# Transposing x raw at the start and loading the output projection's residual from DRAM

## The chip, the core and the metric

One core of a Trainium2 chip runs the kernel. The metric is the device time of one execution in microseconds (us), as the median of several. TensorE (PE in the profile, PEld for its weight loads) multiplies, VectorE (DVE) and ScalarE (ACT) work on tiles and take products out of PSUM, GpSimd (POOL) works on tiles in SBUF, SyncE (SP) issues most of the DMAs. Each engine runs its own list of instructions in order and waits on semaphores.

## The reference

One decoder layer for a prompt of 512 tokens and 64 sample tokens (8 x 8), 1024 channels wide. The mixer's three branches (gated linear attention, pooling, dilated attention) are merged into one product with w_out, and x itself is added to it:

```python
xn = rmsnorm(x, norm1_g)
(q_g, k_g, v_g, r_g, a_lr, u_pool, q_a, k_a, v_a, g_a, g_b, g_c) = split(xn @ w_in)
...
merged = sigmoid(g_a) * y_a + sigmoid(g_b) * y_b + sigmoid(g_c) * y_c
h = x + merged @ w_out
f, c_new = conv_ffn(rmsnorm(h, norm2_g), conv_prev, ffn_w_up, ffn_conv_w, ffn_conv_b, ffn_w_down)
y = rmsnorm(h + f, final_norm_g)
```

All is float32. The outputs are y, the new states and the new key and value caches.

## The kernel before

**Layout.** Activations lie with channels on partitions: a tile [128, 576] holds 128 channels of all 576 tokens (NT; NP = 512 of them are the prompt's). The inputs x lie with tokens on rows, so x is transposed on TensorE. A float32 product is made of three products of float32r parts: weights' high part (wh) by activations' high (xh), wh by low (xl), low (wl) by xh (`products`, line 199; its matmuls are line 207).

**Weights** come in chunks of up to 512 KB, in order of use. `load` (line 145) issues a chunk's DMA on SP into one of three raw slots (wr), `split` (line 154) casts the high part on ACT (line 161) and subtracts the low part on DVE (line 164), for the first two chunks on POOL. `fetch` (line 193) splits chunks i and i + 1 and loads the two after.

**PSUM.** `big` (line 115) gives one of three banks (tag g) for products, `small` (line 123) one of five for the rest (tags s and h).

**Norm 1** (lines 300 to 363). Five tiles xts[t] of 128 tokens (the last of 64) come in by DMA. For each, ACT squares and sums (line 347), POOL makes the reciprocal root (lines 230 and 231), DVE scales the tile in place in two halves of 512 channels (line 351), TensorE transposes each half in four pieces into one PSUM bank (line 354, against the identity, which is the first piece of the constants ca), ACT casts it to xh (line 357) and DVE subtracts to xl (line 358).

**The gate chain** (lines 446 to 475). The low-rank gate's factors (lines 450 and 453) and the first products of k and q are made for tokens 0 to 255 and then for 256 to 575. Logits follow (line 440); the factors reach them over DVE and ACT (lines 455 to 460). ACT takes exponents and logarithms (lines 470 and 472), DVE running sums (line 475). v's products (line 395) are taken out on DVE (line 400, vs), which stands behind the first two of these sums.

**Output projection** (lines 1098 to 1124). x is loaded a second time (lines 1103 and 1104, xt2). For each of eight tiles m of 128 channels five transposes (lines 1110 and 1111) bring x into PSUM, ACT copies it into x1 (lines 1112 and 1113), 48 products follow, and DVE adds half of each product bank to x1 (line 1115). ACT and DVE then make xh2 and xl2, ACT squares (lines 1117 to 1120), POOL sums.

**What sets the order.** The program is written in one sequence; a scheduler places each engine's instructions at build time, by its own estimates, and sets the waits. DMAs on a hardware queue take eight semaphores in turn, so a DMA also waits until the one eight before it has landed. Tiles with `bufs=n` rotate through n slots; a new tenant waits for the last reader of the old.

Of the kernel before, what the change touches and what calls it, by code (L numbers as in the profile page):

```python
# [18 lines left out]
D = 1024  # L19
# [83 lines left out]
def hybrid_step(ctx: ExitStack, tc: tile.TileContext, I, O, at_a, at_b):  # L103
# [3 lines left out]
    # ---------------------------------------------------------------- pools  # L107
# [7 lines left out]
    def big():  # L115
        return psg.tile([128, 512], F32, tag="g", name="g")
# [19 lines left out]
    # ------------------------------------------------------- weight stream  # L136
# [41 lines left out]
    def side_copy(after):  # L178
        """one of the copies within DRAM, issued behind an instruction of the Pool engine"""
        if copies:  # L180
            dst, src = copies.pop(0)
            with tc.issue_after(after.ins):
                nc.gpsimd.dma_start(dst, src)
# [15 lines left out]
    def products(ps, ids, xh, xl, t0, t1, c=0):  # L199
        """weights' hi and lo against the activations' hi and lo, into ps [128, t1 - t0]"""  # L200
# [9 lines left out]
    def gemm(ids, xh, xl, evac, halves=EVEN, c=0, bank=big):  # L210
        """128 columns of x @ w for all tokens, half of them at a time; evac(psum, t0, t1) takes each half away"""
        for t0, t1 in halves:
            ps = bank()
            products(ps, ids, xh, xl, t0, t1, c)
            evac(ps[:, :t1 - t0], t0, t1)

    def tanh_half(t):
        """sigmoid(x) = (1 + tanh(x / 2)) / 2: the tanh"""
        return lambda ps, t0, t1: S.activation(t[:, t0:t1], ps, AF.Tanh, scale=0.5)

    def gate(t):
        """(1 + tanh) x: twice the gated value"""
# [5 lines left out]
    def power(r, ms, e):  # L228
        """r = (ms + e) ** -0.5, two small tiles of one shape"""
# [3 lines left out]
    # ------------------------------------------------------------ constants  # L233
# [14 lines left out]
    # ------------------------------------------------------------ the plan of weight chunks, in order of use  # L248
# [51 lines left out]
    # --------------------------------------------------------------- norm 1  # L300
# [42 lines left out]
    rs = st.tile([128, 5], F32, name="rs")  # L343
    for t in range(5):
        n = 128 if t < 4 else 64
        junk = st.tile([128, D], F32, tag="junk", name="junk", bufs=1)
# [18 lines left out]
    def packed_sample(pool):  # L365
        """[hi | lo] of the samples' activations, one stationary operand"""
# [5 lines left out]
    def token_major(ids, order, out_p, out_s, tmp, xsp):  # L372
        """x @ w for 256 columns with tokens on partitions; out_p [128, 4, 256], out_s [64, 256]."""
# [32 lines left out]
    # ------------------------------------------------------------------ GLA  # L406
# [11 lines left out]
    # the gate's low-rank factors: [hi | hi | lo] against the activations, then [hi; lo; hi] against [hi; hi; lo]  # L418
# [49 lines left out]
    # log gates (times 16) and their running sums within the chunks  # L468
# [10 lines left out]
    def chunked(t, off_p, off_s):  # L479
        """per-chunk element (64 wide chunks, then the samples' 8 wide) broadcast over its chunk"""  # L480
# [13 lines left out]
    for h in range(4):  # L494
# [42 lines left out]
        # the state runs over pairs of chunks: k to the end of the pair, q from its start  # L537
# [11 lines left out]
        # token-major k for the state updates  # L549
# [6 lines left out]
        # the samples', half of them at a time: [hi; hi; lo] of k against [hi; lo; hi] of v  # L556
# [15 lines left out]
        # within the chunks  # L572
# [8 lines left out]
        # between the chunks of a pair  # L581
# [5 lines left out]
        # states after each pair  # L587
# [12 lines left out]
        # the samples' queries against their states  # L600
# [28 lines left out]
        for d in range(2):  # L629
            def silu(ps, t0, t1):  # L630
                """twice the SiLU"""
# [9 lines left out]
        # norm over the head's 256 values, gate  # L641
# [24 lines left out]
    # ------------------------- GLA's gate and projection, and the pooling branch between them  # L666
# [75 lines left out]
    # ------------------------------------------------- the pooling branch's gate and projection  # L742
# [5 lines left out]
    # the FFN's convolution weights and states, channels on partitions  # L748
# [20 lines left out]
    # ---------------------------------------------------------- attention  # L769
# [19 lines left out]
    def minus_max(out, scores, bias, least):  # L789
        """out = -(scores + bias), and its least"""  # L790
        V.tensor_tensor_reduce(out=out, in0=scores, in1=bias, scale=-1.0, scalar=3e38, op0=OP.add, op1=OP.min, accum_out=least)

    def part_scores(g, heads, t, qT, kT):
        """exp(scores - max) of one block of queries; heads as pairs (p, [hh, hh])"""
# [54 lines left out]
    def scores_by_key(g, bq, sp, qb):  # L849
        """every query of a residue against its keys, features on partitions"""  # L850
# [22 lines left out]
    def scores_by_query(sT, bq):  # L873
        """one query to a residue: its row on all partitions, products and sums along the keys' rows"""
# [18 lines left out]
    def sample_units(g, bq):  # L893
        """the samples' attention of one group and half of the batch, in steps"""
# [68 lines left out]
    for g in GROUPS:  # L963
# [38 lines left out]
        # new rows of the caches  # L1002
# [27 lines left out]
    # weights of the groups: softmax over their log-denominators  # L1030
    def group_weights(mxs, dens, shape, pool, tag):
        """mxs (minus m), dens: [128, X, 3, Y] -> weights over sum p v, e^(m - M) / sum den e^(m - M)"""
# [42 lines left out]
    # ------------------------------------------------------------ merge  # L1075
# [22 lines left out]
    # ----------------------------------------------- output projection, norm 2  # L1098
    x1_cm, x1p = open_pool("x1", "right")
    x1 = x1p.tile([128, 8, NT], F32, name="x1")  # L1100
    xr_cm, xrp = open_pool("xr", "right")
    xt = xrp.tile([128, 5, D], F32, name="xt2")
    nc.sync.dma_start(xt[:, :4, :], xin)
    nc.sync.dma_start(xt[:64, 4, :], I["x_sample"].rearrange("b i d -> (b i) d"))
    xh2 = xpool.tile([128, 8, NT], F32R, tag="xh", name="xh2")
    xl2 = xpool.tile([128, 8, NT], F32R, tag="xl", name="xl2")
    for m in range(8):
        px, px2 = small(), small()
        for t in range(4):
            T.transpose(px[:, 128 * t:128 * t + 128], xt[:, t, 128 * m:128 * m + 128], ident)  # L1110
# [187 lines left out]
```

## Time and profile before

| | |
|---|---|
| timed runs, us | 1327.8, 1327.64, 1325.46 |
| median, us | 1327.64 |
| profiled execution, span from first to last instruction, us | 1324.9 |
| TensorE busy, us | 1305.0 |
| DVE, ACT, POOL busy, us | 601.6, 464.3, 242.4 |
| DMA, mean GB/s | 141 |

The page gives no other time for the profiled execution than its span, which lies 2.7 us under the median of the timed runs. Matmuls are pipelined and their busy time runs from the issue to a modelled end, so two that follow each other overlap in the rows; the distance of their starts is what one costs.

### The profile page before, as it was taken

How to read it: one execution, taken by the hardware profiler on the slowest of the kernel's cores; microseconds unless marked ns; L12 is line 12 of the kernel's file. 1: busy time of each engine (PE TensorE's matmuls, PEld its weight loads, DVE VectorE, ACT ScalarE, POOL GpSimd, SP SyncE). 2: the span in 40 equal slices, each digit the busy share in tenths (PEclk: the TensorE clock that was granted, in tenths of full speed). 3: DMA queues.
4: the chain of work that ended last, by engine and by line, in shares of the span. 5: the costliest groups of instructions: out<-in, count | busy, mean ns of one | idle time of the engine just before them, and what ended most of it. 6: DMA issues, size and time to landing. Idle time of an engine off the chain costs nothing.

```text
span 1324.9 us, 23686 instructions
## 1 busy us (share of the span) xinstructions
PE 1305.0 (99%) x9903; PEld 1257.5 (95%) x9903; DVE 601.6 (45%) x1004; ACT 464.3 (35%) x899; POOL 242.4 (18%) x398
## 2 busy tenths in 40 slices
PE   8899999999999999999999999999999999999997
PEld 6899999999999999998988889999999999999997
DVE  5754564433453333162633366435555555532223
ACT  6554553534321222242433343433222222222223
POOL 4320211022410112041311110122121212200000
PEclk9999999999999999999999999999999999999999
DMA  7232432355443557266676415363455555444333
GB/s 218 65 116 68 144 115 69 96 178 158 131 141 95 163 159 220 73 184 190 182 217 204 154 31 167 100 225 118 145 164 162 162 167 157 148 129 149 91 88 116
DMA packets 220582, 187.44 MB, mean 141 GB/s; under 512 B 7900, under 2 KB 216393, under 8 KB 219700
## 3 DMA queue, kind: packets, MB, share of 16 engines
q1 hardware_dynamic: 218682, 142.28, 36.8%
q0 software_dynamic: 1792, 43.65, 9.6%
q8 instruction: 78, 1.28, 0.4%
q14 instruction: 28, 0.23, 0.1%
q10 hardware_dynamic: 2, 0.00, 0.0%
HBM read 175.52 MB, written 54.27 MB: 173 GB/s over the span
## 4 chain that ended last, share of the span: by engine, by line
PE 94%; DVE 2%; ACT 2%; issue 1%; DMA 1%; POOL 0%; SPq 0%; POOLq 0%; DVEq 0%; ACTq 0%
PE g L207 63%; PE g L1249 8%; PE g L395 8%; PE h L1249 2%; PE h L936 1%; PE s L805 1%; PE s L207 1%; PE s L864 1%; PE s L828 1%; PE s L820 1%; PE s L881 1%; PE h L869 1%; PE s L611 0%; DVE bb L475 0%; PE s L591 0%
## 5 line engine op out<-in xcount | busy, mean ns | idle before, releaser
L207 PE MATMUL g<-xl,wh 128*128 128x288 f32 (+2 forms) x1664 | 494.1, 297 | 0.0
L207 PE MATMUL g<-xh,wh 128*128 128x288 f32 (+2 forms) x1664 | 494.1, 297 | 0.0
L207 PE MATMUL g<-xh,wl 128*128 128x288 f32 (+2 forms) x1664 | 492.8, 297 | 1.1 <-DVE wl L164 1.1
L161 ACT CAST wh<-wr 128x1024 fp32r<-128x1024 f32 (+3 forms) x181 | 184.4, 1019 | 485.8 <-PE g L207 287.8
L164 DVE TENSOR_TENSOR wl<-wr,wh 128x1024 fp32r<-128x1024 f32 (+3 forms) x179 | 227.1, 1268 | 252.9 <-ACT wh L161 252.2
L207 PEld LDWEIGHTS g<-xh,wl 128*128 128x128 f32 x1664 | 313.7, 189 | 3.3 <-issue 1.4
L207 PEld LDWEIGHTS g<-xl,wh 128*128 128x128 f32 x1664 | 314.1, 189 | 2.3 <-issue 2.0
L207 PEld LDWEIGHTS g<-xh,wh 128*128 128x128 f32 x1664 | 314.2, 189 | 1.1 <-issue 0.7
L395 PE MATMUL g<-wh,xh 128*128 128x256 f32 x224 | 72.1, 323 | 2.5 <-DVE vs L400 2.5
L1249 PE MATMUL g<-hh,wl 128*128 128x288 f32 (+2 forms) x286 | 72.2, 297 | 0.0
L1249 PE MATMUL g<-hh,wh 128*128 128x288 f32 (+2 forms) x286 | 72.0, 297 | 0.0
L395 PE MATMUL g<-wl,xh 128*128 128x256 f32 x224 | 71.5, 319 | 0.0
L1249 PE MATMUL g<-hl,wh 128*128 128x288 f32 (+2 forms) x286 | 71.5, 295 | 0.0
L395 PE MATMUL g<-wh,xl 128*128 128x256 f32 x224 | 71.4, 320 | 0.0
L395 PEld LDWEIGHTS g<-wh,xh 128*128 128x128 f32 x224 | 52.3, 233 | 5.7 <-DVE vs L400 2.7
L395 PEld LDWEIGHTS g<-wl,xh 128*128 128x128 f32 x224 | 52.3, 234 | 0.7 <-issue 0.7
L395 PEld LDWEIGHTS g<-wh,xl 128*128 128x128 f32 x224 | 52.4, 234 | 0.0
L1249 PEld LDWEIGHTS g<-hh,wl 128*128 128x128 f32 x286 | 49.8, 189 | 0.0
L1249 PEld LDWEIGHTS g<-hh,wh 128*128 128x128 f32 x286 | 49.6, 189 | 0.0
L1249 PEld LDWEIGHTS g<-hl,wh 128*128 128x128 f32 x286 | 49.6, 189 | 0.0
L1159 DVE TENSOR_TENSOR ae<-g,rst 128x256 f32<-128x256 f32 x44 | 18.6, 425 | 64.0 <-PE g L207 64.0
L226 DVE TENSOR_TENSOR yr<-yr,g 128x288 f32<-128x288 f32 x44 | 18.1, 451 | 49.8 <-POOL yr L1189 49.8
(453 smaller groups left out, 2179.9 us busy)
## 6 DMA issues: line engine op xcount, KB each, us to landing
wr<-in_w_in_dram SPq DMA_DIRECT2D x74, 512.0 KB
wr<-in_ffn_w_up_dram SPq DMA_DIRECT2D x44, 512.0 KB
out_dram<-in_cache_k_w_dram POOLq DMA_DIRECT2D x8, 2040.0 KB, 8.4
out_dram<-in_cache_v_w_dram POOLq DMA_DIRECT2D x8, 2040.0 KB, 8.3
kv<-in_cache_k_w_dram SPq DMA_DIRECT2D x26, 512.0 KB
kv<-in_cache_v_w_dram SPq DMA_DIRECT2D x26, 512.0 KB
wr<-in_ffn_w_down_dram SPq DMA_DIRECT2D x18, 448.0 KB
wr<-in_ffn_w_down_dram SPq DMA_DIRECT2D x9, 512.0 KB
```

Of the source, the lines that this page charges most:

```text
L161: S.copy(hi[:, :n], self.raw[:, :n])
L164: self.cut_at = E.tensor_tensor(lo[:, :n], self.raw[:, :n], hi[:, :n].bitcast(F32), op=OP.subtract)
L207: T.matmul(ps[:, :t1 - t0], a[:, k, c:c + 128], b(n)[:, t0:t1], start=(n == 0 and j == 0), stop=(n == len(ks) - 1 and j == 2))
L226: return lambda ps, t0, t1: V.tensor_tensor(t[:, t0:t1], t[:, t0:t1], ps, op=OP.mult)
L395: mm = T.matmul(dst, a, b[:, n % 4, :], start=(n == 0 and j == 0), stop=(n == 7 and j == len(seq) - 1))
L805: T.matmul(sp[:, nk * n:nk * n + nk], qT[r, p, 128 * t:128 * t + 128], kT[r, p, k0:k0 + nk], start=True, stop=True)
L820: T.transpose(pt[:, 128 * n:128 * n + 128], s4[:, h, 128 * kb:128 * kb + 128], ident)
L828: T.matmul(po[64 * hh:64 * hh + 64, 128 * x:128 * x + 128], vt[:, blocks[kb], 64 * (2 * p + hh):64 * (2 * p + hh) + 64], pts[:, (2 * x + h ...
L864: T.transpose(pk[:, 128 * n:128 * n + 128], kt[:, 2 * half + n // 2, 128 * (n % 2):128 * (n % 2) + 128], ident)
L869: T.matmul(sp[32 * b:32 * b + 32, 0:128], qz[:, p, 32 * b:32 * b + 32], kT[:, n, p, :], start=(r == 0 and p == 0), stop=(r == NR[g] - 1 an ...
L1159: V.tensor_tensor(ae[:, 2 + t0:258 + t0], ps[:, :256], rst[:, t0:t0 + 256], op=OP.mult)
L1249: T.matmul(q[:, :t1 - t0], a[:, k, :], b[n][:, t0:t1], start=(n == 0 and j == 0), stop=(n == NF - 1 and j == 2))
```

## The change

At the start each tile xts[t] is also transposed raw, ahead of its scaling: eight more transposes a tile (line 352 of the new kernel) into two of the three product banks, ACT copies the first half and DVE the second (line 353) into a tile xtr with two slots, and SP writes it to a DRAM scratch xturn of [1024, 576] (line 354). Since the scaling works in place, it waits for the raw transposes of its half. At the output projection the second load of x, its 40 transposes and the 16 copies are gone; x1 is now eight tiles, each loaded from xturn (line 1111 of the new kernel). The arithmetic is the same. The other lines of the diff are removed comments, and x1[:, m, ...] written as x1[m][:, ...].

```diff
@@ norm 1, lines 342 to 348 @@
     ss = st.tile([128, 5], F32, name="ss")
     rs = st.tile([128, 5], F32, name="rs")
+
+    xturn = dpool.tile([D, NT], F32, name="xturn")
     for t in range(5):
         n = 128 if t < 4 else 64
+        xtr = st.tile([128, 8, 128], F32, tag="xtr", name="xtr", bufs=2)
+        for kk in range(2):
+            ps = big()
+            for k in range(4):
+                T.transpose(ps[:, n * k:n * k + n], xts[t][:n, 512 * kk + 128 * k:512 * kk + 128 * k + 128], ident[:n, :n])
+            (V.tensor_copy if kk else S.copy)(xtr[:, 4 * kk:4 * kk + 4, :n], ps[:, :4 * n].rearrange("p (k n) -> p k n", k=4))
+        nc.sync.dma_start(xturn.rearrange("(k p) t -> p k t", p=128)[:, :, 128 * t:128 * t + n], xtr[:, :, :n])
         junk = st.tile([128, D], F32, tag="junk", name="junk", bufs=1)
...
@@ output projection, lines 1098 to 1120 @@
     x1_cm, x1p = open_pool("x1", "right")
-    x1 = x1p.tile([128, 8, NT], F32, name="x1")
+    x1 = [x1p.tile([128, NT], F32, name=f"x1_{m}") for m in range(8)]
+    for m in range(8):
+        nc.sync.dma_start(x1[m], xturn[128 * m:128 * m + 128, :])
     xr_cm, xrp = open_pool("xr", "right")
-    xt = xrp.tile([128, 5, D], F32, name="xt2")
-    nc.sync.dma_start(xt[:, :4, :], xin)
-    nc.sync.dma_start(xt[:64, 4, :], I["x_sample"].rearrange("b i d -> (b i) d"))
     xh2 = xpool.tile([128, 8, NT], F32R, tag="xh", name="xh2")
     xl2 = xpool.tile([128, 8, NT], F32R, tag="xl", name="xl2")
     for m in range(8):
-        px, px2 = small(), small()
-        for t in range(4):
-            T.transpose(px[:, 128 * t:128 * t + 128], xt[:, t, 128 * m:128 * m + 128], ident)
-        T.transpose(px2[:, :64], xt[:64, 4, 128 * m:128 * m + 128], ident[:64, :64])
-        S.copy(x1[:, m, :NP], px)
-        S.copy(x1[:, m, NP:], px2[:, :64])
         gemm(P["out", m], lambda k: ga_h[:, k, :], lambda k: ga_l[:, k, :],
-             lambda ps, t0, t1: V.scalar_tensor_tensor(x1[:, m, t0:t1], ps, 0.5, x1[:, m, t0:t1], op0=OP.mult, op1=OP.add))
+             lambda ps, t0, t1: V.scalar_tensor_tensor(x1[m][:, t0:t1], ps, 0.5, x1[m][:, t0:t1], op0=OP.mult, op1=OP.add))
...
```

The scheduler places the rest. Rows of an engine's list name line, operation, output and inputs, and the shape. On TensorE at the very start, before (xt_93 to xt_97 are the tiles of tokens, s and h banks of `small`, g of `big`, ca the identity):

```order
L340 MATMUL s<-grow,ones 128x512 x2
L354 MATMUL s<-ca,xt_93 128x128 x4
L354 MATMUL h<-ca,xt_94 128x128 x4
L354 MATMUL s<-ca,xt_93 128x128 x4
L354 MATMUL s<-ca,xt_94 128x128 x4
L207 MATMUL g<-xh,wh 128x256
L207 MATMUL g<-xl,wh 128x256
```

And now, from the third tile's scaled transposes on (line 352 is raw, line 363 scaled; ahead of these rows stand line 340 and the earlier transposes):

```order
L363 MATMUL s<-ca,xt_95 128x128 x8
L363 MATMUL s<-ca,xt_96 128x128 x4
L352 MATMUL g<-ca,xt_96 128x128 x4
L352 MATMUL g<-ca,xt_97 128x64 x4
L363 MATMUL h<-ca,xt_96 128x128 x4
L352 MATMUL g<-ca,xt_97 128x64 x4
L363 MATMUL s<-ca,xt_97 128x64 x4
L207 MATMUL g<-xh,wh 128x256
```

Products of k and q stood between the transposes of the third to fifth tiles; now all transposes but the last four stand ahead of the first product.

On ACT at the same place, now (line 366 is the cast to xh, line 356 the squares, line 161 a weight cast, line 440 the cast of the gate's gla_wa2, line 515 k's evacuation):

```order
L161 CAST wh<-wr 128x1024
L353 COPY xtr<-g 128x512
L356 ACTIVATE junk,ss<-xt_95 128x1024
L353 COPY xtr<-g 128x512
L356 ACTIVATE junk,ss<-xt_96 128x1024
L356 ACTIVATE junk,ss<-xt_97 64x1024
...
L353 COPY xtr<-g 128x512
L366 CAST xh<-s 128x4x128 x2
L440 CAST wst<-w_355 80x512
L353 COPY xtr<-g 128x512
L366 CAST xh<-h 128x4x128
```

The copy in the last row but one is the fourth tile's. On SP, before and then now (line 430, now 439, is the load of gla_wa2, in three parts; the line-152 load behind it that of the second half of v's weights):

```order
L333 DMA vrows<-in_gla_norm_g_dram 1x256
L430 DMA w_284<-in_gla_wa_dram 16x512 x3
L152 DMA wr<-in_w_in_dram 128x4x256
L511 DMA sg<-in_state_gla_dram 128x8x256
L738 DMA out_dram<-in_state_pool_dram 8x7168
```

```order
L439 DMA w_355<-in_gla_wa_dram 16x512
L354 DMA xturn<-xtr 128x8x128
L439 DMA w_355<-in_gla_wa_dram 16x512
L152 DMA wr<-in_w_in_dram 128x4x256
L439 DMA w_355<-in_gla_wa_dram 16x512
L354 DMA xturn<-xtr 128x8x128
L520 DMA sg<-in_state_gla_dram 128x8x256
L747 DMA out_dram<-in_state_pool_dram 8x7168
L152 DMA wr<-in_w_in_dram 128x8x128
L354 DMA xturn<-xtr 128x8x128 x2
L354 DMA xturn<-xtr 128x8x64
```

The first two writes stand among the gla_wa2 loads, the second behind v's weights; the other three behind the state's load. On SP at the output projection, now:

```order
L152 DMA wr<-in_w_oc_dram 128x6x128 x4
L152 DMA wr<-in_w_out_dram 128x8x128 x5
L1111 DMA x_0_8994<-xturn 128x576
L1111 DMA x_1_8995<-xturn 128x576
L1111 DMA x_2_8996<-xturn 128x576
```

The second load of x stood ahead of the last three w_oc loads; its eight successors stand behind the fifth of the eight w_out loads.

## Rows read from the trace of the kernel before

**Rows 1.** The page: busy time of an engine; the chain that ended last.
```profile
PE 1305.0 (99%) x9903; PEld 1257.5 (95%) x9903; DVE 601.6 (45%) x1004; ACT 464.3 (35%) x899; POOL 242.4 (18%) x398
...
PE 94%; DVE 2%; ACT 2%; issue 1%; DMA 1%; POOL 0%; SPq 0%; POOLq 0%; DVEq 0%; ACTq 0%
```
**Rows 2.** Timeline of PE: start, duration, engine, line, operation, out<-in; output projection's first tile.
```profile
829.25 0.30 PE L207 MATMUL g<-och,wl 128*128 128x288 f32 x1
829.38 0.60 PE L1110 MATMUL h<-ca,xt 128*128 128x128 f32 x4
...
830.12 0.40 PE L207 MATMUL g<-gah,wh 128*128 128x288 f32 x1
830.35 0.29 PE L207 MATMUL g<-gal,wh 128*128 128x288 f32 x1
```
**Rows 3.** Timeline of DVE, the same place; in brackets idle time before, and releaser.
```profile
830.75 1.22 DVE L164 TENSOR_TENSOR wl<-wr,wh 128x1024 fp32r<-128x1024 f32 x1
...
836.19 0.46 DVE L1115 SCALAR_TENSOR_TENSOR x<-g,x 128x288 f32<-128x288 f32 x1 [3.25 <-PE g L207]
```
**Rows 4.** Timeline of SP's DMA issues, 13 to 19 us.
```profile
13.73 3.37 SPq L430 DMA_DIRECT2D w<-in_gla_wa_dram  x3
18.85 0.39 SPq L152 DMA_DIRECT2D wr<-in_w_in_dram  x1
```
**Rows 5.** Waits of SP, 0 to 70 us: total us, times, longest.
```profile
SPq L430 <- DMA wr<-in_w_in_dram: 2.4, 2, 1.2
SPq L152 <- DMA ca<-in_const_a_dram: 1.7, 1, 1.7
```
**Rows 6.** DMA, 18 to 30 us, in 40 slices of 0.3 us.
```profile
GB/s 58 21 0 0 0 0 89 61 143 256 314 375 369 376 386 389 386 362 362 338 355 348 620 649 140 147 227 307 253 213 183 126 32 5 0 0 0 0 0 0
```
**Rows 7.** Timeline of ACT, 9 to 20 us.
```profile
9.49 1.05 ACT L161 CAST wh<-wr 128x1024 fp32r<-128x1024 f32 x1 [0.56 <-DMA wr<-in_w_in_dram]
...
14.44 1.06 ACT L347 ACTIVATE junk<-xt 64x1024 f32<-64x1024 f32 x1
...
15.49 1.04 ACT L161 CAST wh<-wr 128x1024 fp32r<-128x1024 f32 x1
16.48 1.07 ACT L357 CAST xh<-s 128x512 fp32r<-128x512 f32 x2
...
19.85 0.62 ACT L431 CAST wst<-w 80x512 fp32r<-80x512 f32 x1 [1.23 <-DMA w<-in_gla_wa_dram]
```
**Rows 8.** Timeline of DVE: two subtractions from PSUM.
```profile
18.54 1.27 DVE L358 TENSOR_TENSOR xl<-s,xh 128x512 fp32r<-128x512 f32 x2
```
**Rows 9.** Timeline of PE, 10 to 29 us: transposes, and up to the gate's logits.
```profile
10.35 1.11 PE L354 MATMUL h<-ca,xt 128*128 128x128 f32 x4 [1.89 <-DVE xt L351]
...
22.10 0.46 PE L354 MATMUL s<-ca,xt 64*128 64x64 f32 x4
...
22.92 0.65 PE L361 MATMUL s<-ca,vrows 4*128 4x4 f32 x8
...
27.79 0.40 PE L440 MATMUL s<-ast,wst 80*128 80x256 f32 x2
...
28.59 0.39 PE L440 MATMUL s<-ast,wst 80*128 80x256 f32 x1 [0.28 <-DVE a L456]
```
**Rows 10.** Windows of PE: stretch, length, busy (instructions touched), granted clock, DMA share, GB/s.
```profile
13.71:15.41 1.70, 1.70 (x9) 1.00 1.13 317
19.74:21.89 2.15, 2.15 (x19) 1.00 0.82 221
45.40:48.20 2.80, 0.31 (x3) 1.00 0.00 0
49.70:53.10 3.40, 3.40 (x18) 0.50 0.00 0
```
**Rows 11.** Chain in order of time, 27 to 50 us: start, us, what.
```profile
28.05 0.49 DVE a L456
...
47.87 0.31 DVE vs L400
```

More of the change, by code (lines that the diff above doesn't have):

```diff
@@ L1107, in hybrid_step @@
     for m in range(8):
-        px, px2 = small(), small()
-        for t in range(4):
-            T.transpose(px[:, 128 * t:128 * t + 128], xt[:, t, 128 * m:128 * m + 128], ident)
-        T.transpose(px2[:, :64], xt[:64, 4, 128 * m:128 * m + 128], ident[:64, :64])
-        S.copy(x1[:, m, :NP], px)
-        S.copy(x1[:, m, NP:], px2[:, :64])
         gemm(P["out", m], lambda k: ga_h[:, k, :], lambda k: ga_l[:, k, :],
-             lambda ps, t0, t1: V.scalar_tensor_tensor(x1[:, m, t0:t1], ps, 0.5, x1[:, m, t0:t1], op0=OP.mult, op1=OP.add))
+             lambda ps, t0, t1: V.scalar_tensor_tensor(x1[m][:, t0:t1], ps, 0.5, x1[m][:, t0:t1], op0=OP.mult, op1=OP.add))
         g2 = vecs[:, m, 1:2]
-        S.activation(xh2[:, m, :], x1[:, m, :], AF.Copy, scale=g2)
-        V.scalar_tensor_tensor(xl2[:, m, :], x1[:, m, :], g2, xh2[:, m, :].bitcast(F32), op0=OP.mult, op1=OP.subtract)
+        S.activation(xh2[:, m, :], x1[m], AF.Copy, scale=g2)
+        V.scalar_tensor_tensor(xl2[:, m, :], x1[m], g2, xh2[:, m, :].bitcast(F32), op0=OP.mult, op1=OP.subtract)
         sq = xrp.tile([128, NT], F32, tag="sq2" if m else "sqs", name="sq2", bufs=2 if m else 1)
-        S.activation(sq, x1[:, m, :], AF.Square, scale=D ** -0.5)
+        S.activation(sq, x1[m], AF.Square, scale=D ** -0.5)
         if m == 0:
@@ L1216, in rows_out @@
             for n, t in enumerate(ts):
-                T.transpose(px[:r, 128 * n:128 * n + 128], x1[:, m, 128 * t:128 * t + r], ident)
+                T.transpose(px[:r, 128 * n:128 * n + 128], x1[m][:, 128 * t:128 * t + r], ident)
             for n, t in enumerate(ts):
@@ L1250, in down @@
         for q, (t0, t1) in zip(ps, parts):
-            V.tensor_tensor(x1[:, m, t0:t1], x1[:, m, t0:t1], q[:, :t1 - t0], op=OP.add)
+            V.tensor_tensor(x1[m][:, t0:t1], x1[m][:, t0:t1], q[:, :t1 - t0], op=OP.add)
     for m in range(7):
@@ L1255, in hybrid_step @@
         rows_out(m, range(5))
-        side_copy(G.tensor_copy(pace, x1[:, m, 0:1]))
+        side_copy(G.tensor_copy(pace, x1[m][:, 0:1]))
     m = 7
```

## The prediction

> **What bounds the kernel now.** I read the page first: TensorE is busy 99% of the span and makes 94% of the chain of work that ended last [rows 1]. So a time moves the end if it moves the stream of products on TensorE; work on ACT, DVE or the queues counts only where that stream waits for it. I then read two stretches, since the change touches only these: the output projection, and the first 50 us, where the stream starts and the gate chain runs.
>
> In the output projection TensorE goes from the last product of one tile into five transposes and then into the next tile, without a wait [rows 2]. Those transposes are on the path.
>
> At the start the reader should see three things. ACT works through squares, casts of weights and casts of the transposed x, from k's weights at 9.49 to 17.55 us [rows 7]. SP issues its loads one by one, each waiting for a landing: the second half of v's weights, not before 18.85, when the constants have landed [rows 4, 5]. And TensorE fills its waits with products of k and q: the first gate-logit product stands at 27.79 [rows 9], and from there a chain over DVE, ACT and DVE ends in vs at 47.87 [rows 11]. Nothing in that chain hangs on a clock of its own; if its first product moves, all after it moves.
>
> **What goes at the output projection.** Products of 288 columns start 0.13 us apart there: without transposes the next two would start at 829.38 and 829.52. They start at 830.12 and 830.35, the second 0.83 us late [rows 2]. Eight tiles: 8 x 0.83 = **6.6 us off the path**. The 16 ACT copies go too, which nothing waits for, and the old load of x had long landed; both are worth nothing.
>
> The eight new loads stand on SP behind the load of the fifth w_out chunk, which waits for DVE's low part of the second chunk, done at 831.97 [rows 3]. From v's load, issued at 18.85, the bytes flow at the full 375 GB/s some 1.6 us later, and 512 KB take 1.4 us [rows 4, 6]. So the chunk is through at about 835.0, x1's first tile (288 KB, 0.8 us) at 835.8, seen at about 836.6. Its first reader is DVE's addition, at 836.19 before and 0.8 earlier now [rows 3]. DVE would wait 1.2 us. Behind it on DVE stand the low part of the next chunk and xl2, both with microseconds in hand. TensorE has a third product bank and takes the first half of the next tile into it, 24 products or 3.2 us; only then does it need the bank that DVE holds. So I cost this at 0; without that bank it would cost the 1.2 us once. The later tiles follow each 0.8 us, and are needed each 6.4 us. The next w_out load waits behind these eight; it has over 10 us.
>
> **What comes at the start.** The orders show it. Before, TensorE took products as soon as the first two tiles were in; now no product of k stands ahead of the last raw transposes. TensorE takes its work in order, so the first product waits for the slowest of them. I follow that back.
>
> The last raw transposes write the product bank from which ACT copies the fourth tile's first half. That copy needs xtr's second slot, so the second tile's write to DRAM must have landed. On SP that write now stands behind the load of v's second half. The load cannot go before 18.85 [rows 4, 5]: issuing it takes 0.39, the gla_wa2 load between them no longer, so the write is issued at about 19.7. The second tile's copies are done long before, so nothing but SP holds it. Its bytes come behind v's 512 KB: 18.85 + 1.6 + 1.4 + 1.4 = 23.3. A landing is seen later: the third gla_wa2 load was seen at 19.85 [rows 7], while the stream had run dry by about 18.6 [rows 6]; between 0.3 and 1.2, I take 0.9. So **24.2**. Behind ACT's waiting copy stand its casts of the last tiles; DVE's copy of the other half waits for the same landing, with the fifth tile's scaling behind it; TensorE waits for both. Then ACT's copy, priced like its cast of the same shape from PSUM, 1.07 for two, 0.53 [rows 7]; then four raw and four scaled transposes of 64 columns. Four transposes take 0.46 at the quick pace and 1.11 at the slow one [rows 9], of which the next instruction waits for some 0.4 or 0.9; I take 0.8 each, since TensorE has mostly idled by then. The first product stands at 24.2 + 0.55 + 1.6 = **26.4**.
>
> From there to the first gate-logit product: 48 products, at 2.15 us for 18 starts [rows 10] 5.7; the last four transposes 0.4; the stretch 22.92 to 27.79 less one product [rows 9] 4.75; together 10.9. On top comes the pace. From 49.7 the granted clock was 0.50 for 3.4 us, the lower level of 1.2 GHz, TensorE having idled for most of 45.4 to 48.2; at the first products the column reads 1.00, but 8 starts took 1.70 us, 0.213 each for 0.119 [rows 10]. Slow products for 1.7 us lose 0.75, for 3.4 us 1.5; I take 1.3, nearer the long one, because TensorE waits more now. Sum: 26.4 + 10.9 + 1.3 = 38.6, against 27.79: **10.8 us later**. Some 0.5 comes back: the last logit product waited until 28.59 for DVE's sum [rows 9, 11], and the sums of the first half now stand before q's products. So 10.3.
>
> What hangs on ACT alone bounds this from below. ACT's list from k's cast at 9.49 to that copy is now two weight casts, three squares, seven casts of x, three copies and the gate's cast: 2 x 1.0 + 3 x 1.05 + 10 x 0.53 + 0.6 = 11.05 [rows 7], so 20.5 without one wait. With quick transposes the first product is at 21.9, the logits at 32.8, 5.0 later, 4.5 after the 0.5: **-2.1 us** in all. From above: at half of 375 GB/s each write takes 1.4 longer, two stand before 24.2, so +2.7; at a third, +5.6. The nearest row is the load at 375, with rows of the same 512 bytes, so I take that. DVE's five copies cost 0.64 each, priced like its subtraction from PSUM [rows 8]; those that matter end before the copy that waits. The last three writes stand on SP ahead of weight loads that wait for a slot of the ring anyway.
>
> **The sum.** +10.3 - 6.6 = **+3.7 us**. The page gives the profiled execution a span of 1324.9 and no other time, so 1328.6 there; the median of the runs shown lies 2.7 above that span, and carried to it the time is 1327.6 + 3.7 = **1331.3 us**. Faster or slower below means by over 0.2%, 2.65 us, about what a measurement of this kernel can tell from no change.
>
> The pace is the open term. The trace of before shows its first products slow too, behind transposes [rows 9, 10], and does not settle whether dense transposes would have raised it. If they do, the 1.3 goes and the two groups of transposes take 0.4 instead of 0.8 each: +1.6, 1329.2.
>
> The Trainium skill, "TensorE: Matmul & The Clock Gate", section "Part 4: PE-mode transpose", says that transposes do not count as busy for the clock gate as products do. By that rule the slow pace is certain and the sum stays at +3.7; a quick pace from the first product on would speak against it.
>
> **Rivals.**
> 1. *The start hides it* (not slower). The writes land early or the pace is quick, so that ACT's own list sets the first product. For it: before, the first products stood before 13.71 [rows 10], so there is time to hide in, and the floor worked out above is -2.1. Against it: the 18.85 that SP waits for is a row, not a guess. It decides from a first product before about 25.0: a first product at 24.3 at the quick pace gives 24.3 + 10.9 - 27.79 - 0.5 - 6.6 = +0.3. Times 1325.5 to 1329; I put it at **1328**.
> 2. *The write is slow.* Half the rate of the loads gives +6.4, **1334**; a third gives +9.3, 1337, and there the third tile's write also begins to hold the fifth tile's copy, which stands on ACT ahead of the gate's casts. For it: five writes of 512-byte rows share the stream with a 1 MB state load. Against it: the loads of the same packets ran at 375.
> 3. *x1 arrives late.* If its first tile is seen after about 838.5 instead of 836.6, TensorE stops in the second tile, one for one. Up to +2: **1333**.
> 4. *Faster.* The edit at the projection in full, and the waits at 45 to 56 us absorb most of the delay: they lie behind the gate chain, which starts from the delayed product, so nothing in the trace offers this; to reach **1324**, seven of the ten microseconds would have to vanish.
>
> That the change does not do what it says is no case: the order holds none of the forty transposes at the projection.
>
> **Chances.** Forecast (+1.5 to +6) 0.52; rival 1 0.30; rival 2 0.11; rival 3 0.03; rival 4 0.04. Of the forecast's 0.52 about 0.10 lies under +2.65. So slower 0.42 + 0.11 + 0.03 = 0.56; same 0.30 + 0.10 less 0.02 for a low tail = 0.38; faster 0.04 + 0.02 = 0.06. The range runs from near the floor, 1326.0, to near the case of a third, 1336.5.
>
> **What would show it.** The projection's tiles should repeat every 6.4 us instead of 7.2, with no idle on TensorE. In the first 40 us: ACT's copy of the fourth tile waiting for a DMA until about 24; the first product of k at about 26 instead of before 13.71; the first gate-logit product at about 38.6; vs some 10 later. A first product before 24, or logits before 35, makes the forecast wrong towards no change; a write landing after 26 makes it wrong the other way.

## The result

| kernel | timed runs, us | median, us | profiled span, us |
|---|---|---|---|
| before | 1325.46 to 1327.8 (4 runs) | 1326.97 | 1324.9 |
| after | 1332.54 to 1336.81 (4 runs) | 1333.52 | 1330.8 |

The change makes the kernel slower. The medians differ by 6.55 us; the ratio of the runs is 1.0057, 95% interval 1.0043 to 1.0071, which is 7.6 us with an interval of 5.7 to 9.4. The profiled spans differ by 5.9; the profiled execution of the changed kernel is the fastest of its four (1332.54). The forecast was 1331.3, and slower as the likeliest sign.

The page still shows TensorE as the bound, with 0.4 us more of busy time than in [rows 1] and a smaller share of the chain:

```profile
PE 1305.4 (98%) x9903; PEld 1258.3 (95%) x9903; DVE 603.8 (45%) x1009; ACT 462.6 (35%) x888; POOL 244.6 (18%) x398
...
PE 92%; DVE 2%; ACT 2%; DMA 1%; issue 1%; SPq 1%; POOL 0%; POOLq 0%; DVEq 0%; ACTq 0%
```

So the time is not in work but in waits, and in a slow pace behind one of them. I followed the distance between the two traces along the span, by the same instruction in both: +11.1 at the gate's chain, +12.2 after the pooling branch, +5.5 after the output projection, +5.9 at the end. Three places make it.

**The start, +11.1.** SP's issues, then ACT's copies, then TensorE, in the kernel after (line 353 copies to xtr, 354 writes xturn, 352 transposes raw, 363 scaled, 440 casts the gate's factors, 449 makes the logits). SP and ACT (start, duration, engine, line, what; in brackets idle time and releaser):

```profile
19.26 0.38 SPq L152 DMA_DIRECT2D wr<-in_w_in_dram  x1
19.70 0.49 SPq L439 DMA_DIRECT2D w<-in_gla_wa_dram  x1
20.30 0.38 SPq L354 DMA_DIRECT2D xturn<-xtr  x1
```

```profile
20.64 0.59 ACT L353 COPY xtr<-g 128x512 f32<-128x512 f32 x1 [0.60 <-DMA xturn<-xtr]
...
23.35 0.62 ACT L440 CAST wst<-w 80x512 fp32r<-80x512 f32 x1 [0.80 <-DMA w<-in_gla_wa_dram]
25.00 0.59 ACT L353 COPY xtr<-g 128x512 f32<-128x512 f32 x1 [1.03 <-DMA xturn<-xtr]
```

```profile
13.60 0.60 PE L352 MATMUL g<-ca,xt 128*128 128x128 f32 x4
...
16.90 1.08 PE L363 MATMUL s<-ca,xt 128*128 128x128 f32 x4 [2.70 <-DVE xl L367]
...
25.64 0.46 PE L352 MATMUL g<-ca,xt 64*128 64x64 f32 x4 [1.36 <-ACT xtr L353]
25.94 0.41 PE L363 MATMUL s<-ca,xt 64*128 64x64 f32 x4
26.28 0.43 PE L207 MATMUL g<-xh,wh 128*128 128x256 f32 x1
...
38.91 0.40 PE L449 MATMUL s<-ast,wst 80*128 80x256 f32 x2
...
39.71 0.38 PE L449 MATMUL s<-ast,wst 80*128 80x256 f32 x1 [0.28 <-DVE a L465]
```

The reader is to see a chain that goes from queue to engine to engine: the second write is issued behind v's load, at 20.30; ACT's copy of the fourth tile waits for it until 25.00; the last raw transposes wait for that copy until 25.64; the first product of k stands at 26.28, the first gate-logit product at 38.91 for 27.79 [rows 9]. From the first product on the products are slow. The windows (stretch, length, busy, granted clock, DMA share, GB/s), with the columns of PE, PEld, DVE, ACT and POOL between:

```profile
14.20:16.90 2.70, 0.00 (x0) 0.03 (x1) 1.86 (x4) 2.67 (x7) 1.57 (x4) 0.88 1.11 372
16.25:23.05 6.80, 5.52 (x23) 4.05 (x24) 5.26 (x9) 4.52 (x8) 2.62 (x2) 0.50 0.89 277
23.10:26.45 3.35, 1.67 (x16) 1.23 (x16) 2.72 (x5) 1.76 (x4) 1.26 (x1) 1.00 1.07 343
26.50:29.85 3.35, 3.35 (x17) 3.35 (x17) 1.30 (x3) 0.25 (x1) 0.00 (x0) 0.50 1.11 344
30.83:38.90 8.07, 8.07 (x69) 7.25 (x69) 2.09 (x6) 4.13 (x10) 0.00 (x0) 1.00 0.36 94
```

TensorE stood for the 2.7 us before 16.90, and up to 23 the granted clock is 0.50, the lower of its two levels, 1.2 GHz. From 23.1 to 26.4 it is 1.00 again; in that stretch TensorE stands 1.36 us for ACT's copy, and from 26.5, as the products start, the clock is 0.50 once more until 29.9. The 24 products from 26.28 to 30.83 take 4.55 us; at 0.12 each they would take 2.88. That is 1.7 us. The chain of waits then carries the delay on, unchanged, to vs, which stood at 47.87 [rows 11]:

```profile
58.99 0.31 DVE vs L409
```

**The pooling branch, +1.1.** This was not foreseen. TensorE transposes the first rows of the pool's state (stl) and waits for their load; the first row is of the kernel before, the second of the one after:

```profile
268.76 0.32 PE L684 MATMUL s<-ca,stl 120*128 120x120 f32 x1 [0.55 <-DMA stl<-in_state_pool_dram]
```

```profile
280.96 0.32 PE L693 MATMUL s<-ca,stl 120*128 120x120 f32 x1 [1.62 <-DMA stl<-in_state_pool_dram]
```

**The projection, -6.7.** TensorE goes from one product to the next where [rows 2] had 0.83 us of transposes, and DVE waits for x1's first tile alone:

```profile
841.42 0.29 PE L207 MATMUL g<-och,wl 128*128 128x288 f32 x1
841.56 0.29 PE L207 MATMUL g<-gah,wh 128*128 128x288 f32 x1
```

```profile
849.44 0.82 DVE L1117 SCALAR_TENSOR_TENSOR x<-g,x 128x288 f32<-128x288 f32 x2 [4.33 <-DMA x<-xturn]
```

TensorE doesn't wait for that: its products follow each other every 0.13 us through 851. The first row of [rows 2], at 829.25, stands at 841.42 now, 12.2 later; the first sums over the squares behind the projection, 887.22 before, stand at 892.67, 5.5 later:

```profile
887.22 0.28 PE L1128 MATMUL s<-ones,sq 128*128 128x1 f32 x2
```

```profile
892.67 0.28 PE L1130 MATMUL h<-ones,sq 128*128 128x1 f32 x2
```

The sum by the trace is 11.1 + 1.1 - 6.7 = 5.5. The 0.4 that the spans differ by beyond that lies behind the projection, and I have not traced it.

### The profile page after: what moved, and what is told of

It reads as the page before. It is cut to its first block, busy times and chain, and to the rows that moved or that the text cites. A ratio compares the mean times of both kernels' runs of the same rounds, so it can differ in the third digit from the quotient of the medians.

```text
span 1330.8 us, 23717 instructions
## 1 busy us (share of the span) xinstructions
PE 1305.4 (98%) x9903; PEld 1258.3 (95%) x9903; DVE 603.8 (45%) x1009; ACT 462.6 (35%) x888; POOL 244.6 (18%) x398
## 4 chain that ended last, share of the span: by engine, by line
PE 92%; DVE 2%; ACT 2%; DMA 1%; issue 1%; SPq 1%; POOL 0%; POOLq 0%; DVEq 0%; ACTq 0%
PE g L207 62%; PE g L1251 8%; PE g L404 8%; PE s L1251 2%; PE h L945 1%; PE s L814 1%; PE s L207 1%; PE s L873 1%; PE s L837 1%; PE s L829 1%; PE s L890 1%; PE h L878 0%; PE s L620 0%; DMA xt<-in_x_prompt_dram 0%; DVE bb L484 0%
```

## The experiments

Theory: the start's landing, not its work, sets the first product; the pooling wait is a thing of its own; the projection's gain is whole. Rivals stand with each run. All intervals are 95%, against runs of the kernel before on the same chip.

### Each half alone

One kernel has the start of the change and the projection of before, the other the start of before and the projection of the change.

```diff
@@ start_alone, against the change @@
-        nc.sync.dma_start(x1[m], xturn[128 * m:128 * m + 128, :])
+    xt = xrp.tile([128, 5, D], F32, name="xt2")      # and the loads, transposes and copies of before
@@ proj_alone, against the change @@
-    xturn = ...                                       # and all of lines 347 to 354
-        nc.sync.dma_start(x1[m], xturn[128 * m:128 * m + 128, :])
+        nc.sync.dma_start(x1[m], xrows[r0:r0 + 128, :])
```

> The start of the change (raw transposes, copies, five writes to the scratch), but the output projection of before, with its second load of x and its 40 transposes; nothing reads the scratch. Theory: the two parts add up. The start costs what vs is later in the profile of the changed kernel, 58.99 for 47.87, plus the 1.1 us lost at the pooling branch: +12.2, so 1339 us. Rival: part of the start's delay is caught up by later waits and it is the projection that pays less than its 6.6; then this kernel is at +8 to +9, 1335 to 1336.

> The start of before, and the projection of the change: no transposes, no second load of x, eight tiles x1 loaded one by one. No transposed x exists then, so x1 is loaded from x's rows as they lie, with rows of 576 elements as in the change; the residual is therefore not x. Theory: 8 x 0.83 = 6.6 us off the path and nothing put on it, 1320.3 us, and no pooling wait either. Rival: the first tile's addition waits for its load and the product banks do not cover all of it: -5.5, 1321.5 us.

Measured: the start alone 1339.95 us, ratio 1.0101 (1.0088 to 1.0115), +13.4 by the ratio; the projection alone 1320.8, ratio 0.9958 (0.9945 to 0.9970), -5.6, where -6.7 lies inside the interval. The two add to +7.8, and the change has +7.6 (5.7 to 9.4) by the ratio. The parts add up within what the runs can tell; that the second alone falls short of 6.7 has a reason of its own, told with the control below. The rival of the first run, a delay that is caught up later, falls: vs stands at 59.80 with the start alone. The pooling wait belongs to the start. First the row with the start alone, then with the projection alone, which has none:

```profile
281.65 0.32 PE L693 MATMUL s<-ca,stl 120*128 120x120 f32 x1 [1.50 <-DMA stl<-in_state_pool_dram]
```

```profile
269.92 0.32 PE L685 MATMUL s<-ca,stl 120*128 120x120 f32 x1
```

### What sets the first product

A third slot for xtr lets the fourth tile's copy go with the first write's landing:

```diff
-        xtr = st.tile([128, 8, 128], F32, tag="xtr", name="xtr", bufs=2)
+        xtr = st.tile([128, 8, 128], F32, tag="xtr", name="xtr", bufs=3)
```

> The changed kernel with three slots for xtr for two, so that the copy of the fourth tile waits for the landing of the first write (seen at 20.64 in the profile of the change) and not of the second (24.94). Theory, that this landing sets the first product: first product of k at 22 to 22.5 for 26.34, first gate-logit product about 35 for 38.91, total 3.5 to 4 less than the change, 1329.5 to 1330 us. Rival, that ACT's own list sets it, with the cast of the gate's factors that waits for a landing at 23.35: first product near 25, 1.3 less, 1332 us.

Measured: 1327.8 us, ratio 1.0005 (0.9994 to 1.0017), the same as before. By the ratios the change's +7.6 has shrunk to +0.7 (by the medians, +6.55 to +1.7), by more than the theory gave. ACT's copy, and TensorE:

```profile
20.25 0.59 ACT L353 COPY xtr<-g 128x512 f32<-128x512 f32 x1 [1.57 <-DMA xturn<-xtr]
```

```profile
13.50 1.06 PE L363 MATMUL s<-ca,xt 128*128 128x128 f32 x4
...
15.20 0.60 PE L363 MATMUL h<-ca,xt 128*128 128x128 f32 x4
15.64 1.63 PE L352 MATMUL g<-ca,xt 128*128 128x128 f32 x12
...
19.36 1.25 PE L363 MATMUL s<-ca,xt 128*128 128x128 f32 x8 [1.31 <-DVE xt L360]
...
22.12 0.36 PE L207 MATMUL g<-xh,wh 128*128 128x256 f32 x1
...
33.63 0.40 PE L449 MATMUL s<-ast,wst 80*128 80x256 f32 x2
```

The first product is where the theory put it, 22.12, and the gate's factors, cast at 23.05 here, don't hold it: the rival falls. The first logit product is at 33.63, not 35, because the products run at the quick pace from the first one on. So of the 5.3 us won at the logits 4.2 are the landing; the rest is the pace, 1.7, less 0.6 that the stretch behind the first product takes longer. The rows also show what the trace of before left open: TensorE had done nothing but transposes since 6.0, and from 15.20 on four of them take 0.6 instead of 1.1, with starts 0.11 apart instead of 0.21. Transposes alone raised the pace. The column of the granted clock can't show this step: it reads 1.00 here both from 10.9 to 15.1 and from 15.2 to 21.7, so in the first 15 us only the distance of the starts tells. The quick pace lasted over a pause of 1.31; in the change the clock fell to 0.50 in the pause of 2.70, and again behind one of 1.36, so the length of a pause alone doesn't tell.

The Trainium skill, "TensorE: Matmul & The Clock Gate", section "Part 4: PE-mode transpose", has it that in transpose mode the clock gate's full clock doesn't engage. Whether these run in that mode the rows don't say, which call them MATMUL. For them the trace says otherwise, and the measurement decides.

### The queue of the writes

The writes go to POOL's queue, with two slots as in the change:

```diff
-        nc.sync.dma_start(xturn.rearrange("(k p) t -> p k t", p=128)[:, :, 128 * t:128 * t + n], xtr[:, :, :n])
+        nc.gpsimd.dma_start(xturn.rearrange("(k p) t -> p k t", p=128)[:, :, 128 * t:128 * t + n], xtr[:, :, :n])
```

> The changed kernel with the five writes issued by POOL in place of SP, two slots for xtr as in the change. SP's list is that of before again. Theory, that the place on SP behind the load of v's second half made the write late: the second write is issued near 15.5 for 20.30, lands near 20, the gate's factors land at 19.85 as before; first product 22 to 23, first gate-logit product about 34.5, total about 4 less than the change, 1329.5 us. Rival, that POOL pays: its reciprocal roots and weight subtractions stand behind the writes' waits, tiles are scaled later, no gain: 1333 us or more.

Measured: 1335.08 us, ratio 1.0064 (1.0051 to 1.0078): no gain. The writes do go early, and ACT's copies of the third and fourth tile don't wait for a landing any more, yet the first product stands at 29.22. POOL, then ACT:

```profile
13.08 1.15 POOL L354 DMA_DIRECT2D xturn<-xtr  x1
...
15.22 0.98 POOL L354 DMA_DIRECT2D xturn<-xtr  x1
```

```profile
21.45 0.62 ACT L440 CAST wst<-w 80x512 fp32r<-80x512 f32 x1 [3.09 <-DMA w<-in_gla_wa_dram]
...
24.96 1.08 ACT L353 COPY xtr<-g 128x512 f32<-128x512 f32 x2
```

The scheduler, which saw another order of landings, put the cast of the gate's factors ahead of three casts and a copy of x that stand before it in the change, and ACT stood 3.09 us for those factors' load; the granted clock is 0.50 from 20.7 to 34.2. So this run doesn't test the place of the write: it replaced one wait at the head of ACT's list by another. It shows how this start breaks, by whichever landing stands at the head of ACT's list.

### The pooling wait

Where does it come from? The writes could have moved the queue's semaphores, the copies could have moved ACT, or TensorE's own list could matter: 40 transposes that stood at the projection now stand ahead. This kernel is the one before with 40 idle transposes of 4 columns:

```diff
     pv = small()
+    for k in range(40):
+        T.transpose(pv[:, 4 * k:4 * k + 4], vrows[:, 4 * k:4 * k + 128], ident[:4, :4])
     for k in range(8):
```

> The kernel before with 40 more transposes of 4 columns at line 361 (22.92 in its profile), written over by the eight that stand there, and with nothing else changed on any engine or queue. It asks for the 1.1 us at the pooling branch: there the changed kernel waits 1.62 for the first load of the pool state, before 0.55, and in the trace of the change a fetch of instructions of 0.02 MB (queue q8) stands at 276.0 to 276.5, beside that load's bytes, where before it stands at 271.0, 2.5 us behind them. Theory: the 40 raw transposes ahead of it are 40 more instructions with 40 more weight loads on TensorE, so its fetches come earlier in the work; 40 small ones do the same, and the wait is 1.5 to 1.6 here too. Rival, that the writes or loads on SP, the copies on ACT or DVE, or where data lies make it: 0.5 as before. In either case some 3 us longer for the 40 transposes' own time.

Measured: 1332.82 us in one run, 6.7 more than before: 3.7 stand at the first gate-logit product (31.45), 1.5 are told with the control below, and the wait is there, with no write, no copy and no other order:

```profile
22.48 2.66 PE L361 MATMUL s<-ca,vrows 4*128 4x4 f32 x40
...
274.93 0.32 PE L686 MATMUL s<-ca,stl 120*128 120x120 f32 x1 [1.55 <-DMA stl<-in_state_pool_dram]
```

So the number of TensorE's instructions ahead of it makes the wait. What stands beside the load is a fetch of instructions, one packet of 0.02 MB on queue q8. In half-microsecond windows of the DMA view (queue: packets, MB, share of 16 engines) it stands at 276.0 in the change, where the load was issued at 275.74, at 271.0 in this kernel, where it was issued at 269.79, and at 271.0 before, 2.2 us after TensorE had the data. The change's row:

```profile
q8 instruction: 1, 0.02, 15.6%
```

0.156 x 16 x 0.5 = 1.25 us of one DMA engine, about the wait gained. All eleven traces, those of the kernels below too, say the same. In the eight with 40 more transposes ahead of the branch the fetch starts within 1.6 us of the load's issue, and the wait is 1.27 to 1.83; in the three without (before, the projection alone, the control below) it starts 6.5 us behind the issue, and the wait is 0 to 0.55. The page counts 78 of these packets for 9903 products and transposes, one for every 127, and they keep to TensorE's list: the fourteenth starts when 1726 to 1728 have begun, in all eleven traces. So 40 more move the fetches by about a third of their distance, here onto the load. That the load's own part on that engine stands behind the packet is the likely way: with the start alone the last packets ahead of 281.0 run for a microsecond at 7.2 and 7.3% of 16 engines, about one engine, where before there are none from 268.5 to the end of the wait. That it is the engine of the fetch no row shows.

### The raw transposes in an idle stretch

[rows 10] show TensorE idle for most of 45.4 to 48.2, and slow behind it. Four kernels ask whether the transposes fit there. In the first, the scaling writes into tiles of its own and leaves x, and the transposes stand in v's products of the first head:

```diff
-            V.scalar_tensor_tensor(xk, xk, rs[:n, t:t + 1], gb1[kk][:n], op0=OP.mult, op1=OP.mult)
+            xk = s2.tile([128, 512], F32, tag="xk", name="xk", bufs=3)
+            V.scalar_tensor_tensor(xk[:n], xts[t][:n, 512 * kk:512 * kk + 512], ...)
...
+                        if between and t == 2 and n == 0 and j == 0:
+                            mm, first = between(mm), True      # 40 raw transposes behind mm, 10 ACT copies, one write
```

> The projection of the change, but the raw transposes stand in v's products of the first head, between the third and the fourth group of tokens, where TensorE stood idle from 45.7 to 48.2 before: into the banks of the small products, ACT copies them, one write to the scratch. For that the scaling writes into tiles of its own and leaves x as it is. The low-rank chain is as before. DVE's addition vs moves ahead of the second running sum by it. Theory: 40 transposes at 0.11 are 4.4 us, of which 2.5 lie in the idle stretch and 1.5 come back since the clock does not fall behind it; ACT's first copies stand behind v's casts, so TensorE waits 1 to 2 for a bank: the start costs 1 to 2 us, with the pooling wait 2 to 3; less 6.7 that is 4 us less than before, 1322.5 us. Rival, that the chain behind (gates, POOL, the weights' subtraction on DVE) takes on all that ACT and TensorE do there: +5 at vt, no gain, 1326 us.

Measured: 1328.23 us, ratio 1.0012 (1.0002 to 1.0021), for 1322.5 expected, and above the rival's 1326 too. TensorE waits for ACT's copies, which the scheduler had put behind v's casts, 0.54 and then the 1.94 of this row, and the granted clock is 0.50 from 51.8 to 58.5:

```profile
51.43 1.73 PE L486 MATMUL s<-ca,xt 128*128 128x128 f32 x8 [1.94 <-ACT xtr L487]
```

In the second, ACT takes five copies first:

```diff
+                    with tc.issue_after(xc[4]) if between else nullcontext():   # xc: the copies of x
                         S.copy(out_p[:, 0:2].rearrange("p b c -> p (b c)"), ps[1])
```

The same stands at v's casts and at one exponential.

> As the kernel named late, but ACT takes the first five copies ahead of v's copies and casts (44.9 to 47.5, where ACT stood idle before). Theory: no bank is waited for, all transposes are through at about 50, and the start costs no more than 1 us with the clock's return, with the pooling wait 2; 1321.5 us. Rival: what comes later on ACT, v's casts and the last products' copies, holds the chain: 1323 us or more.

Measured: 1323.05 us, ratio 0.9975 (0.9965 to 0.9985), some 3 us less than before, for 1321.5 expected. No bank is waited for, and TensorE stands nowhere from 42 to 75; what is lacking stands ahead of that, with the first gate-logit product at 29.91 for 27.79. The third is the control, the new order without the transposes and with the projection of before:

> The kernel before with the new order of the kernel named late (vs ahead of the second running sum, scaling into own tiles), but without the raw transposes, the write and the loads of x1: the projection is that of before. It tells what the order alone is worth. Theory: TensorE's idle stretch at 45.7 goes, 2.5 us, and the slow products behind it, 1.5, but the wait for the weights' subtraction at 55.9 takes most of it back: 0 to -2, 1325 us. Rival: nothing takes it back: -4, 1322 us.

Measured: 1329.98 us, ratio 1.0025 (1.0014 to 1.0035), slower, against both of my theories. The order differs from what I expected: without the transposes the scheduler left vs behind the second sum, and TensorE stood 2.52 us at 49 as before, so this run says nothing on vs. The first logit product is at 28.55, so the scaling into own tiles loses some 0.8 here; why it stands at 28.89 and 29.91 in the two kernels above, with the same scaling, is open. And the slow stretch has moved. v's products ran at full clock behind that pause, TensorE reached the next wait, for the weights' low part, earlier, stood there 2.55 us for 1.07 before, and was slow behind it:

```profile
56.66 0.40 PE L207 MATMUL g<-xh,wl 128*128 128x288 f32 x1 [2.55 <-DVE wl L164]
```

```profile
50.00:54.00 4.00, 4.00 (x34) 3.87 (x33) 3.94 (x7) 2.87 (x5) 3.81 (x4) 1.00 0.00 0
54.00:58.00 4.00, 1.45 (x11) 1.34 (x11) 3.80 (x4) 1.42 (x3) 2.79 (x3) 0.99 0.04 10
58.00:62.00 4.00, 4.00 (x23) 3.65 (x23) 2.02 (x4) 1.31 (x4) 0.00 (x0) 0.58 0.87 257
```

This is not the new order's doing. Kernels whose lists are alike at this place divide in two: the slow stretch lies behind the first pause, and the second is 1.1 long, in the kernel before, the change, the start alone and the one with POOL's queue; it lies behind the second, 2.55 long, in the projection alone, with three slots, with the 40 small transposes and here. Between vs and the pooling branch the second kind loses 1.5 us more: with three slots 8.4 - 5.9 - 1.1 = 1.4 (the distances to before at the branch and at vs, and the pooling wait), with the small transposes 6.2 - 3.7 - 1.0 = 1.5. In the first kind the slow stretch costs nothing: from the product behind the first pause to the one behind the second it is 7.67 in both (48.24 to 55.91 before, 48.37 to 56.04 with the projection alone), for DVE's low part sets the second, and the time lost only shortens that wait. That accounts for what the projection alone lacks to 6.7, and part of what the control loses; where its remainder lies I have not traced.

The fourth kernel gives up the tiles of its own. The start is that of before, in place, and POOL loads x a second time at 23:

```diff
+    with tc.issue_after(wlow.ins):                   # wlow: the last of the gate's factors, line 433
+        nc.gpsimd.dma_start(xt[:, :4, :], xin)
+        nc.gpsimd.dma_start(xt[:64, 4, :], xsam)
```

> As the kernel named late2, but the start is that of before, instruction for instruction: x is scaled in place, and for the raw transposes POOL loads it a second time after the gate's factors, from about 22 on, while the queues run dry at 28 to 34. In late2 the first gate-logit product stood at 29.91 for 27.79 before. Theory: that start was lost by the scaling into tiles of its own, and is back here: first gate-logit product near 27.8, the transposes in the place of TensorE's idle stretch, the start costs 0 to 0.5, the pooling wait 1.1 to 1.3, the projection gains 6.7: 5 less than before, 1321 us. Rival: the second load of x, 2.3 MB, pushes the loads of v's and r's weights, and the products of v wait: 1323 us, as late2, or more.

Measured: 1320.55 us, ratio 0.9957 (0.9943 to 0.9970), 5.7 less than before; it beats both kernels. TensorE, then its windows:

```profile
27.11 0.40 PE L446 MATMUL s<-ast,wst 80*128 80x256 f32 x2
...
44.18 1.91 PE L492 MATMUL s<-ca,xt 128*128 128x128 f32 x16
...
269.14 0.32 PE L722 MATMUL s<-ca,stl 120*128 120x120 f32 x1 [1.72 <-DMA stl<-in_state_pool_dram]
```

```profile
44.00:46.00 2.00, 2.00 (x20) 2.00 (x20) 2.00 (x4) 1.31 (x4) 1.72 (x1) 1.00 0.00 0
46.00:48.00 2.00, 2.00 (x20) 1.83 (x19) 2.00 (x3) 1.85 (x4) 1.89 (x2) 1.00 0.00 0
48.00:50.00 2.00, 2.00 (x21) 1.93 (x20) 2.00 (x5) 1.52 (x4) 1.93 (x3) 1.00 0.00 0
50.00:54.00 4.00, 4.00 (x35) 4.00 (x35) 2.28 (x4) 2.18 (x7) 3.92 (x4) 1.00 0.31 121
```

No pause, and a granted clock of 1.00 where [rows 10] had 0.50. The rival falls: v's products wait for no load. At the pooling branch, with 1.2 us more of its wait, the kernel stands 0.4 behind the one before (269.14 for 268.76); 0.7 it was ahead already at the first gate-logit product (27.11 for 27.79), which no run explains. Between the two places, less the pooling wait, the kernels take the same within 0.1: the transposes have cost nothing there that the trace shows. There was room for their 4.2 us: before, TensorE stood 2.52 and 1.07 between 45 and 56 and lost 1.5 to the slow pace, 5.1 in all. That they fill a stretch that was idle and then slow is shown by the windows; how much of that is theirs and how much belongs to vs, which moved ahead of the second sum in this order, these runs don't part.

## Why the prediction was right, and where its terms were off

**Right: the sign, the mechanism, the range.** The start costs more than the projection gives, and the time lies in 1326.0 to 1336.5. The time was 2.2 low. The difference, 3.7, was 1.8 low against the trace's 5.5 and 2.9 against the medians' 6.55, and some of the steps were met by luck, as told below.

| step | forecast | measured |
|---|---|---|
| projection's gain | 6.6 | 6.7 |
| x1's first tile, carried to the new times | seen at 848.8, DVE waits 1.2, TensorE 0 | 849.44, some 1.9, 0 |
| second write issued | 19.7 | 20.30 |
| its landing seen | 24.2 | 24.94 |
| from there to the first product | 2.2 | 1.3 |
| first product of k | 26.4 | 26.28 |
| loss by the slow pace | 1.3 | 1.7 |
| first gate-logit product | 38.6 | 38.91 |
| given back by DVE's sum | 0.5 | 0 |
| start in all | 10.3 | 11.1 |
| pooling branch | none | 1.1 |
| sum | +3.7 | +5.5 by the trace; timed +6.55 by the medians, +7.6 (5.7 to 9.4) by the ratio |

For the table: x1's forecasts are 836.6 and the addition at 835.4, each 12.2 later.

**The write's issue.** v's load went at 19.26 instead of 18.85, which is most of the 0.6; the gla_wa2 load behind it, priced at no more than 0.39, stands at 19.70 with 0.49. The write itself took 4.63 us from issue to seen, for 4.5 worked out:

```profile
20.30 4.63 DMA xturn<-xtr
```

The errors of this stretch cancelled, and that 26.28 came so near 26.4 is luck: the landing was 0.7 late, and the last two groups of transposes needed 0.64 from their start to the first product where 1.6 was allowed. The 0.8 for each was taken from two rows of [rows 9] that differ in shape: 0.46 is four transposes of 64 columns, 1.11 four of 128. The groups here are of 64, and the granted clock was 1.00; four of 64 at the slow pace took 0.69 in the kernel with POOL's queue, at 28.61.

**The 0.5 given back** is the step that was wrong in kind. The last logit product waits for DVE's addition of the second half's sum (the row [0.28 <-DVE a L465] above answers to the last of [rows 9]), and that sum's products stand directly ahead of the logits in both kernels. What I took to be early now was the first half's.

**The pooling wait** is the term that no step had. The sum put what lies between the gate chain and the projection at nothing because no edit of the change lies there; the wait came by TensorE's instruction count, and cost 1.1.

**The pace** was named as the open term and had the right sign: the products were slow, and it cost 1.7 for 1.3. The reason given for 1.3, that TensorE waits more now, fits the rows: the clock fell at 26.5, with 1.36 us of waiting just ahead. The doubt whether dense transposes raise the pace is settled: with three slots they did. In the change too the clock was at 1.00 again from 23.1 on; that it fell just as the products began is nothing that the trace of before could have told.

**Rivals.** The first, that the start hides, was priced at 1328 if the writes land early or the pace is quick; with three slots both held, and it measured 1327.8. So it was the right alternative, and one slot parts it from what happened. That its number is met is luck: by the rival's own sum a first product at 22.12 gives 22.1 + 10.9 - 27.8 - 0.5 - 6.6 = -1.9, and the pooling wait and the moved slow stretch, which it did not have, added 1.1 and 1.4. The second, a slow write, did not hold: 4.63 us is what the loads' rate gave. The row it was priced by was misread: the load of v's weights moves rows of 1 KB (353 packets for 0.35 MB from 21 to 22 before), not of 512 bytes. It made no difference: from 22 to 24 in the change 1168 packets, some 570 bytes each, went at 335 GB/s. The third did not occur. The fourth, faster, needed the delay to vanish behind the gate chain, and the start alone shows that all of it comes through.

## What to carry to other kernels

A step moved to the start of a kernel is paid by the landing at the head of an engine's list, not by its work: look for the slot whose release waits for a DMA, and for what else that engine has queued behind it; one more slot was worth 5.3 us at the gate's logits here, and 4.8 to 6.9 in the timed runs. Work for an engine that is busy 99% is free only where it is idle, so read the idle stretches first and put the work there by hand: the same 40 transposes that took 6.6 us at the projection, and with their writes made the start 11 us later, left the kernel no later at 44 us, where TensorE and the slow pace had left 5.1 us of room. And a pause has a second price behind it, the slow clock, that can fall at one of two places from kernel to kernel and move a result by 1.5 us, a good part of what such a change is worth.

## What the runs showed of the hardware

- A fetch of TensorE's instructions, one packet of 0.02 MB that holds a DMA engine for 0.9 to 1.4 us, beside a load of 120 KB goes with some 1.1 us more of waiting for that load: 1.27 to 1.83 in eight traces with the fetch beside the load, 0 to 0.55 in three without. Forty transposes more or fewer ahead of the place switch it on or off.
- Transposes of float32 alone, 128 x 128, brought TensorE from 0.21 us a transpose to 0.11. A pause of 1.31 us left it there (three slots); the granted clock fell to 0.50 in a pause of 2.70 and behind one of 1.36 (the change), and behind one of 2.55 (the control). Of two pauses that follow each other at 46 and 55 us, one has a slow stretch of some 3.4 us behind it, the first in four traces and the second in four.
- A write that POOL issued took 0.89 to 1.15 us of POOL itself; the same write on SP 0.38.
